# Splitting the mixers' weights ahead of time: hi and lo halves made during the feed-forwards, kept in DRAM and loaded back

## The chip, the cores and the metric

The kernel runs on one NeuronCore of a Trainium2 chip. Its engines work side by side, each through its own queue in order: TensorE (PE in the profile) multiplies matrices into the accumulators in PSUM, VectorE (DVE), ScalarE (ACT) and GpSimd (POOL) work element by element, and SyncE (SP) issues all the DMA transfers of this kernel. The metric is the device time of one execution in microseconds, as the median of several runs.

## What is computed

Two decoder layers on 512 tokens of width 1024. Each layer adds half a SwiGLU feed-forward, a token mixer, and half a second feed-forward to the residual x. Layer 0 mixes with retention and dilated attention side by side ("hybrid"), layer 1 with stick-breaking attention ("stick").

```python
def swiglu_ffn(x, g, w_in, w_out):
    h = rms_norm(x, g)
    gate, up = jnp.split(h @ w_in, 2, axis=-1)
    return (jax.nn.silu(gate) * up) @ w_out          # w_in 1024 x 5632, w_out 2816 x 1024
...
for layer in range(DEPTH):
    x = x + 0.5 * swiglu_ffn(x, ffn1_norm[layer], ffn1_w_in[layer], ffn1_w_out[layer])
    if layer % 2 == 0:
        x = x + retention_dilated_mixer(x, mix_norm[layer], hyb_w_in[e], ret_gn[e], hyb_w_out[e])
    else:
        x = x + stick_breaking_mixer(x, mix_norm[layer], sb_w_in[o], sb_w_out[o])
    x = x + 0.5 * swiglu_ffn(x, ffn2_norm[layer], ffn2_w_in[layer], ffn2_w_out[layer])
return rms_norm(x, final_norm)
```

All is float32. The mixers' inner parts (rotary embedding, decay, softmax, cumulative log-sums) are written out in the kernel; for this change only their projections with `hyb_w_in`, `hyb_w_out`, `sb_w_in` and `sb_w_out` matter.

## The kernel before

**Three products for one.** Each float32 operand of a projection is cut into a high part, rounded to the matmul type fp32r, and a low part, the rest. `mm3` (L139) then issues three matmuls per 128 x 128 block of weights: hi by hi (L141), hi by lo (L142), lo by hi (L143). Activations lie transposed in SBUF, 128 features by 512 tokens a tile, already split (`hh`, the `o` chunks, the feed-forward's `us`).

**A unit of weights** is a tile of 128 partitions by up to 1024 columns. `weight` (L121) makes one: SP loads the raw tile (`wraw`, four buffers), ACT casts it into `hi` (`whi`, two buffers, L128), and an engine subtracts, lo = raw - hi (`wlo`, two buffers, L129). That engine is `lo_eng[0]`: VectorE in the feed-forwards, GpSimd in the two mixers (L688 and L695 switch to it, L690 and L697 back). A full unit of 1024 columns feeds 24 matmuls of 512 columns.

**Order of the stages:** feed-forward 1 of layer 0, `hybrid`, feed-forward 2 of layer 0, feed-forward 1 of layer 1, `stick`, feed-forward 2 of layer 1. A feed-forward is `ffn` (22 steps f, each a gate unit and an up unit with 24 matmuls apiece, silu, product, split of the result into `u`) and `out_ffn` (8 steps d, each with three units of 8, 7 and 7 blocks, the residual add L215 and the next norm L175).

**A mixer** starts with projections (`hybrid`: four gate units `hyb_g`; `stick`: the first q and k) and then runs eight head pairs. `prep(i+1)` projects q, k and, every second pair, v of the next pair; q and k of the hybrid go through `qk_rot` (L437: a shuffle of the PSUM result L441, products L443 and L444, a sum L445) and are packed by `pack_q` (L392, with ACT L399, L400 and DVE L401) and `pack_k` (L376, DVE L381 and L382). Then the core of pair i runs: `retention_core` (scores into PSUM at L409, times decay at L470, split at L146 and L147), `dilated_core` (softmax with L508, L512, transposes L519), or `stick_core` (ACT L593 and L90, DVE L596, split L151 and L152, then matmuls L617). `attend` (L411) multiplies with the values at L420 and adds the halves at L425. `out_mix` (L279) projects the outputs with 8 units of 640 columns and 4 of 768. GpSimd also splits the output chunks' lo (L152 from `split_v`) and scales the rotary tables (L452); these are not touched.

**Order in the queues.** The program is a plain unrolled Python trace. A planner orders each engine's queue from program order, estimated durations and the buffers that are free, and sets every semaphore; no order is written by hand around the change.

Of the kernel before, what the change touches and what calls it, by code (L numbers as in the profile page):

```python
# [20 lines left out]
P = 128  # L21
# [13 lines left out]
def trunk(ctx: ExitStack, tc: tile.TileContext, a: dict, out: bass.AP):  # L35
    nc = tc.nc
    cpool = ctx.enter_context(tc.tile_pool(name="cpool", bufs=1))
    wraw = ctx.enter_context(tc.tile_pool(name="wraw", bufs=4))
    whi = ctx.enter_context(tc.tile_pool(name="whi", bufs=2))
    wlo = ctx.enter_context(tc.tile_pool(name="wlo", bufs=2))  # L40
    hpool = ctx.enter_context(tc.tile_pool(name="hpool", bufs=1))
    big = ctx.enter_context(tc.tile_pool(name="big", bufs=1))
    tmp = ctx.enter_context(tc.tile_pool(name="tmp", bufs=1))
# [77 lines left out]
    def weight(src, cols, pieces=None):  # L121

        raw = wraw.tile([P, 1024], F32, tag="wraw", name=nm("wraw"))
        hi = whi.tile([P, 1024], F32R, tag="whi", name=nm("whi"))
        lo = wlo.tile([P, 1024], F32R, tag="wlo", name=nm("wlo"))
        if pieces is None:
            nc.sync.dma_start(raw[:, :cols], src)
            nc.scalar.copy(out=hi[:, :cols], in_=raw[:, :cols])  # L128
            lo_eng[0].tensor_tensor(out=lo[:, :cols], in0=raw[:, :cols], in1=f32(hi[:, :cols]), op=ALU.subtract)  # L129
        else:  # L130
            for c0, c1, then in pieces:
                nc.sync.dma_start(raw[:, c0:c1], src[:, c0:c1])
                then()
            for c0, c1, _ in pieces:
                nc.scalar.copy(out=hi[:, c0:c1], in_=raw[:, c0:c1])
                nc.vector.tensor_tensor(out=lo[:, c0:c1], in0=raw[:, c0:c1], in1=f32(hi[:, c0:c1]), op=ALU.subtract)
        return hi, lo

    def mm3(ps, whl, col, rhs_hi, rhs_lo, first, last):  # L139
        h, l = whl  # L140
        nc.tensor.matmul(ps, h[:, col:col + P], rhs_hi, start=first, stop=False)  # L141
        nc.tensor.matmul(ps, h[:, col:col + P], rhs_lo, start=False, stop=False)  # L142
        nc.tensor.matmul(ps, l[:, col:col + P], rhs_hi, start=False, stop=last)  # L143
# [51 lines left out]
        return hpool.tile([P, SEQ], F32, tag="ss", name=nm("ss"))  # L195

    def proj_tile(src, ps, w=None):
        w = w or weight(src, D)
        for k in range(KC):
            mm3(ps, w, k * P, hh[k][:, 0, :], hh[k][:, 1, :], k == 0, k == KC - 1)  # L200

# [13 lines left out]
        nc.vector.scalar_tensor_tensor(out=x[d][:, sl], in0=ps[:, sl], scalar=0.5, in1=x[d][:, sl],  # L215
                                       op0=ALU.mult, op1=ALU.add)

    def out_ffn(w_out, us, gcol):

        ss = norm_start()  # L220
        act_set(LNEXP)
        for d in range(KC):
            ps = ACC()
            out_tile(w_out[d], ps, us)
            add_half(d, ps)
            norm_chunk(d, gcol, ss)
# [52 lines left out]
    def out_mix(wa, wb, chunks, gcol):  # L279

        ss = norm_start()
        for d in range(KC):
            ps = ACC()
            w = weight(wa[d], 640)
            for f in range(5):
                mm3(ps, w, f * P, chunks[f][:, 0, :], chunks[f][:, 1, :], f == 0, f == 4)
            nc.vector.tensor_add(out=x[d], in0=ps, in1=x[d])
        for d in range(KC):
            if d % 2 == 0:
                w = weight(wb[d // 2], 768)  # L290
            ps = ATT()
            for f in range(3):
                mm3(ps, w, (d % 2) * 384 + f * P, chunks[5 + f][:, 0, :], chunks[5 + f][:, 1, :], f == 0, f == 2)
            nc.vector.tensor_add(out=x[d], in0=ps, in1=x[d])
            norm_chunk(d, gcol, ss)
        return ss

    def ffn(r, w_in, first=None, pieces=None):

        us = []  # L300
        for f in range(FC):
            pg = ACC()
# [29 lines left out]
    def values(wsrc, rtm):  # L332

        pv = [ACC(), ACC()]
        for u in range(2):
            h, l = weight(wsrc[u], 1024)
            for kk in range(4):
                k = 4 * u + kk
                wh, wl = h[:, kk * 256:kk * 256 + 256], l[:, kk * 256:kk * 256 + 256]
                for t in range(NB):  # L340
                    hi, lo = hh[k][:, 0, t * P:(t + 1) * P], hh[k][:, 1, t * P:(t + 1) * P]
                    o = pv[t // 2][:, (t % 2) * 256:(t % 2) * 256 + 256]
                    nc.tensor.matmul(o, hi, wh, start=k == 0 and t % 2 == 0, stop=False, skip_group_check=True)  # L343
# [186 lines left out]
    def hybrid(ss, gcol_next):  # L530
        gates = []
        for p in range(4):
            ps = ACC()
            proj_tile(a["hyb_g"][p], ps)
            if p == 0:
                r = norm_r(ss)
                rtm = token_r(r)
                act_set(SILU)
            g = T()
            nc.vector.tensor_mul(out=g, in0=ps, in1=r)  # L540
            if p % 2 == 0:
# [10 lines left out]
        def prep(i):  # L552
            p = i % 4
            if i < 4:
                if p % 2 == 0:
                    vs[i // 2] = values(a["hyb_rv"][p // 2], rtm)
                return (qk_rot(a["hyb_rq"][p], rot_r, sw_r, pack_q), qk_rot(a["hyb_rk"][p], rot_r, sw_r, pack_k))
            if p % 2 == 0:
                vs[i // 2] = values(a["hyb_dv"][p // 2], rtm)
            return (qk_rot(a["hyb_dq"][p], rot_d, sw_d, lambda y: pack_q(y, -0.125)),  # L560
                    qk_rot(a["hyb_dk"][p], rot_d, sw_d, pack_k))

        ready = prep(0)
        for i in range(8):
# [7 lines left out]
                retention_core(i, q, k, vs[i // 2], gates[i], outs, bd)  # L572
            else:
                dilated_core(i - 4, q, k, vs[i // 2], dmask, outs)
        return out_mix(a["hyb_oa"], a["hyb_ob"], outs, gcol_next)

    def stick_core(p, q, k, v, cm, outs, idr, tri, nones):
        banks = {}
# [53 lines left out]
        outs.append(oo)  # L632

    def stick(ss, gcol_next):
        first = [project(a["sb_q"][0]), project(a["sb_k"][0])]
        r = norm_r(ss)
        rtm = token_r(r)
        r8 = T(tag="r2")
# [9 lines left out]

        def prep(p, ps=None):
            if p and p % 2 == 0:  # L650
                vs[p // 2] = values(a["sb_v"][p // 2], rtm)
            qp, kp = ps or (project(a["sb_q"][p]), project(a["sb_k"][p]))
            return qk_plain(qp, r8, pack_q), qk_plain(kp, r, pack_k)

        ready = prep(0, first)
        vs[0] = values(a["sb_v"][0], rtm)
        for p in range(8):
            q, k = ready
            if p < 7:
# [23 lines left out]
            norm_sum(c, ss)  # L683
        return norm_r(ss)

    us = ffn(sums, a["f1_in"][0], first, [(c, c + 512, lambda: None) for c in (0, 512)])
    ss = out_ffn(a["f1_out"][0], us, 8)
    lo_eng[0] = nc.gpsimd  # L688
    ss = hybrid(ss, 16)
    lo_eng[0] = nc.vector  # L690
    us = ffn(lambda: norm_r(ss), a["f2_in"][0])
    ss = out_ffn(a["f2_out"][0], us, 24)
    us = ffn(lambda: norm_r(ss), a["f1_in"][1])
    ss = out_ffn(a["f1_out"][1], us, 32)
# [130 lines left out]
```

## Time and profile before

| what | value |
|---|---|
| median of 3 runs | 2083.76 us (2082.23 to 2086.93) |
| the profiled execution's own time | 2081.9 us |
| its span, first to last instruction | 2080.0 us |
| feed-forward 1, layer 0 | to about 373 us |
| hybrid mixer | about 373 to 687 us |
| the two feed-forwards between the mixers | about 687 to 1412 us |
| stick mixer | about 1412 to 1712 us |
| feed-forward 2, layer 1 | from about 1712 us |
| raw loads of 512 KB, issue to landing | 3.4 us |
| HBM read / written | 182.88 MB / 2.10 MB |

A span of the profile counts from the first instruction; the execution's own time has 1.9 us around it. In the rows of a window, "PE busy (x)" is busy time with the number of instructions that start there; two instructions in flight at once count once. Matmuls overlap: one is listed with about 390 ns but a new one of 512 columns starts about every 227 ns, so the pace of TensorE is read from the count in a stretch that it fills.

### The profile page before, as it was taken

To read this page: it belongs to the slowest core of one execution; us is meant where nothing else is said; L and a number is where in the kernel's file an instruction comes from. 1 tells how busy PE (TensorE), PEld (TensorE's weight loads), DVE (VectorE), ACT (ScalarE), POOL (GpSimd) and SP (SyncE) were. 2 spreads that over 40 slices of the span, in tenths; PEclk is the share of its full clock that TensorE was granted. 3 is DMA by queue.
4 is the path that set the end of the run, shared out by engine and by line. 5 is a ranking of instruction groups with operands and counts; after the bars stand their busy time and mean duration, and the time that the engine had idled before them with its cause. 6 is when DMAs were issued, how large, how long until landed. Compare 5 with 4: busy or idle time off the path is not lost.

```text
span 2080.0 us, 23646 instructions
## 1 busy us (share of the span) xinstructions
PE 1999.6 (96%) x9440; PEld 1662.7 (80%) x9440; DVE 1113.3 (54%) x1640; ACT 769.8 (37%) x1124; POOL 196.4 (9%) x104
## 2 busy tenths in 40 slices
PE   8999999987889999999999999999898999999997
PEld 7888888876667788888888888888777778888887
DVE  6444433378987644443344444336777874444334
ACT  5323332334445423233233323225655653232323
POOL 0000000532223000000000000003322220000000
PEclk9999999999999999999999999999999999999999
DMA  5223333312112332333332323332111032223333
GB/s 183 100 93 100 95 94 100 116 62 71 58 35 71 102 101 92 101 88 100 97 101 91 102 96 92 101 97 75 61 42 46 28 100 91 100 93 101 93 92 125
DMA packets 55695, 186.51 MB, mean 90 GB/s; under 512 B 6304, under 2 KB 7072, under 8 KB 55584
## 3 DMA queue, kind: packets, MB, share of 16 engines
q1 hardware_dynamic: 55584, 185.00, 28.0%
q8 instruction: 74, 1.21, 0.2%
q14 instruction: 37, 0.30, 0.0%
HBM read 182.88 MB, written 2.10 MB: 89 GB/s over the span
## 4 chain that ended last, share of the span: by engine, by line
PE 84%; DVE 12%; ACT 3%; issue 1%; DMA 0%; SPq 0%; DVEq 0%; ACTq 0%
PE acc L142 18%; PE acc L143 18%; PE acc L141 18%; PE att L141 8%; PE att L142 8%; PE att L143 8%; PE att L617 2%; PE po L420 2%; DVE qk L381 1%; ACT t L90 1%; DVE tp L444 1%; PE acc L345 1%; PE acc L344 1%; PE acc L343 1%; DVE qk L382 1%
## 5 line engine op out<-in xcount | busy, mean ns | idle before, releaser
L128 ACT CAST whi<-wraw 128x1024 fp32r<-128x1024 f32 (+3 forms) x352 | 356.3, 1012 | 1007.9 <-PE acc L142 550.4
L129 DVE TENSOR_TENSOR wlo<-wraw,whi 128x1024 fp32r<-128x1024 f32 (+1 forms) x276 | 328.5, 1190 | 238.9 <-ACT whi L128 236.9
L141 PE MATMUL acc<-h,whi 128*128 128x512 f32 x992 | 390.6, 394 | 6.0 <-ACT h L174 6.0
L142 PE MATMUL acc<-h,whi 128*128 128x512 f32 x992 | 389.8, 393 | 0.9 <-DVE h L175 0.6
L143 PE MATMUL acc<-h,wlo 128*128 128x512 f32 x992 | 390.0, 393 | 0.0
L129 POOL TENSOR_TENSOR wlo<-wraw,whi 128x1024 fp32r<-128x1024 f32 (+2 forms) x76 | 167.4, 2202 | 1436.6 <-ACT whi L128 1376.8
L141 PE MATMUL att<-h,whi 128*128 128x512 f32 x704 | 275.1, 391 | 0.0
L143 PE MATMUL att<-h,wlo 128*128 128x512 f32 x704 | 274.3, 390 | 0.0
L142 PE MATMUL att<-h,whi 128*128 128x512 f32 x704 | 273.9, 389 | 0.0
L141 PEld LDWEIGHTS acc<-h,whi 128*128 128x128 f32 x992 | 187.8, 189 | 44.9 <-ACT h L174 5.9
L142 PEld LDWEIGHTS acc<-h,whi 128*128 128x128 f32 x992 | 187.7, 189 | 41.1 <-DVE h L175 3.6
L143 PEld LDWEIGHTS acc<-h,wlo 128*128 128x128 f32 x992 | 187.6, 189 | 39.0 <-issue 0.7
L315 DVE TENSOR_TENSOR tp<-att,r 128x512 f32<-128x512 f32 x88 | 60.9, 692 | 281.4 <-PE att L143 281.4
L309 DVE TENSOR_TENSOR tp<-acc,r 128x512 f32<-128x512 f32 x88 | 60.9, 692 | 183.6 <-PE acc L143 183.4
L141 PEld LDWEIGHTS att<-h,whi 128*128 128x128 f32 x704 | 132.3, 188 | 28.0 <-issue 0.7
L142 PEld LDWEIGHTS att<-h,whi 128*128 128x128 f32 x704 | 132.0, 188 | 27.9 <-issue 0.7
L143 PEld LDWEIGHTS att<-h,wlo 128*128 128x128 f32 x704 | 132.1, 188 | 27.8 <-issue 0.2
L141 PE MATMUL acc<-o,whi 128*128 128x512 f32 (+1 forms) x352 | 135.3, 384 | 0.0
L142 PE MATMUL acc<-o,whi 128*128 128x512 f32 (+1 forms) x352 | 134.8, 383 | 0.0
L143 PE MATMUL acc<-o,wlo 128*128 128x512 f32 (+1 forms) x352 | 134.3, 382 | 0.0
L141 PEld LDWEIGHTS acc<-o,whi 128*128 128x128 f32 x352 | 66.5, 189 | 11.7
L142 PEld LDWEIGHTS acc<-o,whi 128*128 128x128 f32 x352 | 66.5, 189 | 11.7
(179 smaller groups left out, 2960.0 us busy)
## 6 DMA issues: line engine op xcount, KB each, us to landing
wraw<-f_in SPq DMA_DIRECT2D x174, 512.0 KB, 3.4
wraw<-f_out SPq DMA_DIRECT2D x68, 448.0 KB, 3.3
wraw<-f_out SPq DMA_DIRECT2D x34, 512.0 KB, 3.5
wraw<-sb_q SPq DMA_DIRECT2D x8, 512.0 KB, 3.4
wraw<-sb_k SPq DMA_DIRECT2D x8, 512.0 KB, 3.4
wraw<-sb_v SPq DMA_DIRECT2D x8, 512.0 KB, 3.4
wraw<-hyb_oa SPq DMA_DIRECT2D x8, 320.0 KB, 2.8
wraw<-sb_oa SPq DMA_DIRECT2D x8, 320.0 KB, 2.8
```

Of the source, the lines that this page charges most:

```text
L90: r = nc.scalar.activation(out=o, in_=i, func=f, **kw)
L128: nc.scalar.copy(out=hi[:, :cols], in_=raw[:, :cols])
L129: lo_eng[0].tensor_tensor(out=lo[:, :cols], in0=raw[:, :cols], in1=f32(hi[:, :cols]), op=ALU.subtract)
L141: nc.tensor.matmul(ps, h[:, col:col + P], rhs_hi, start=first, stop=False)
L142: nc.tensor.matmul(ps, h[:, col:col + P], rhs_lo, start=False, stop=False)
L143: nc.tensor.matmul(ps, l[:, col:col + P], rhs_hi, start=False, stop=last)
L309: nc.vector.tensor_mul(out=t1, in0=pg, in1=rr)
L315: nc.vector.tensor_mul(out=t2, in0=pu, in1=rr)
L343: nc.tensor.matmul(o, hi, wh, start=k == 0 and t % 2 == 0, stop=False, skip_group_check=True)
L344: nc.tensor.matmul(o, hi, wl, start=False, stop=False, skip_group_check=True)
L420: nc.tensor.matmul(po[:, SEQ - n:], st, banks[b][:, c, at:at + n], start=j == 0 and c == 0, stop=j == NB - 1 and c == 1, skip_group_check= ...
L617: nc.tensor.matmul(z[:, at + n - m:at + n], st, sp[:, c, s0:s0 + m], start=False, stop=i == len(adds) - 1 and c == 1, skip_group_check=True)
```

## The change

During the first three feed-forwards each step also makes one unit of the next mixer's weights (`cut_ahead`): the usual load, cast on ACT and subtraction on VectorE, and then two DMA writes, of hi and of lo, into a DRAM tile. In the mixers `unit` finds such a tile and `weight_cut` loads it: in turn into one `whl` buffer with one DMA, or into two `wraw` buffers with two DMAs. The pools `whi` and `wlo` (two buffers each of 4 KB a partition) become one pool `whl` of three buffers that hold hi and lo together (8 KB).

28 hybrid units (all but its output projection) are cut in the first feed-forward, at steps f = 2 to 21 of `ffn` and d = 0 to 7 of `out_ffn`; all 36 stick units in the next two, 18 in each `ffn`. The hybrid's 12 output units still go through `weight`; as `lo_eng` is not switched any more, VectorE subtracts them. GpSimd keeps its other work.

```diff
-    whi = ctx.enter_context(tc.tile_pool(name="whi", bufs=2))
-    wlo = ctx.enter_context(tc.tile_pool(name="wlo", bufs=2))
+    whl = ctx.enter_context(tc.tile_pool(name="whl", bufs=3))
+    dram = ctx.enter_context(tc.tile_pool(name="dram", bufs=1, space=bass.MemoryType.DRAM))
...
-        hi = whi.tile([P, 1024], F32R, tag="whi", name=nm("whi"))
-        lo = wlo.tile([P, 1024], F32R, tag="wlo", name=nm("wlo"))
+        hl = whl.tile([P, 2, 1024], F32R, tag="whl", name=nm("whl"))
+        hi, lo = hl[:, 0, :], hl[:, 1, :]
...
+    def cut_ahead(key, cols):
...
+        hi, lo = weight(src, cols)
+        keep = dram.tile([P, 2, cols], F32, tag="cut_" + "_".join(map(str, key)), name="cut_" + "_".join(map(str, key)))
+        for i, part in enumerate((hi, lo)):
+            nc.sync.dma_start(keep[:, i, :], f32(part[:, :cols]))
+        cut[key] = keep
...
+    def weight_cut(key, cols):
...
+        turns[0] += 1
+        keep = cut[key]
+        if turns[0] % 2:
+            hl = whl.tile([P, 2, 1024], F32R, tag="whl", name=nm("whl"))
+            nc.sync.dma_start(f32(hl[:, :, :cols]), keep)
+            return hl[:, 0, :], hl[:, 1, :]
+        hl = [wraw.tile([P, 1024], F32R, tag="wraw", name=nm("wcut")) for _ in range(2)]
+        for i in range(2):
+            nc.sync.dma_start(f32(hl[i][:, :cols]), keep[:, i, :])
+        return hl
+
+    def unit(key, cols):
+        if key in cut:
+            return weight_cut(key, cols)
...
             norm_chunk(d, gcol, ss)
+            if ahead:
+                cut_ahead(*ahead.pop(0))
...
             us.append(u)
+            if ahead and f > 1:
+                cut_ahead(*ahead.pop(0))
...
-    us = ffn(sums, a["f1_in"][0], first, [(c, c + 512, lambda: None) for c in (0, 512)])
-    ss = out_ffn(a["f1_out"][0], us, 8)
-    lo_eng[0] = nc.gpsimd
+    us = ffn(sums, a["f1_in"][0], first, [(c, c + 512, lambda: None) for c in (0, 512)], hyb)
+    ss = out_ffn(a["f1_out"][0], us, 8, hyb)
     ss = hybrid(ss, 16)
-    lo_eng[0] = nc.vector
-    us = ffn(lambda: norm_r(ss), a["f2_in"][0])
+    half = sb[:18]
+    us = ffn(lambda: norm_r(ss), a["f2_in"][0], ahead=half)
     ss = out_ffn(a["f2_out"][0], us, 24)
-    us = ffn(lambda: norm_r(ss), a["f1_in"][1])
+    half = sb[18:]
+    us = ffn(lambda: norm_r(ss), a["f1_in"][1], ahead=half)
     ss = out_ffn(a["f1_out"][1], us, 32)
-    lo_eng[0] = nc.gpsimd
     ss = stick(ss, 40)
-    lo_eng[0] = nc.vector
```

In the mixers each call `weight(a["sb_q"][p], ...)` and the like becomes `unit(("sb_q", p), ...)`; `hyb` and `sb` list the units in the order of their use.

More of the change, by code (lines that the diff above doesn't have):

```diff
@@ L137, in weight, with mm3 @@
         return hi, lo
-    def mm3(ps, whl, col, rhs_hi, rhs_lo, first, last):
-        h, l = whl
+    cut = {}
+    def cut_ahead(key, cols):
+        src = a[key[0]]
+        for i in key[1:]:
+            src = src[i]
+        hi, lo = weight(src, cols)
[3 more added lines that the diff above has]
+        cut[key] = keep
+    turns = [0]
+    def weight_cut(key, cols):
[12 more added lines that the diff above has]
+            return weight_cut(key, cols)
+        src = a[key[0]]
+        for i in key[1:]:
+            src = src[i]
+        return weight(src, cols)
+    def mm3(ps, w, col, rhs_hi, rhs_lo, first, last):
+        h, l = w
         nc.tensor.matmul(ps, h[:, col:col + P], rhs_hi, start=first, stop=False)
@@ L197, in proj_tile @@
     def proj_tile(src, ps, w=None):
-        w = w or weight(src, D)
+        w = w or (unit(src, D) if isinstance(src, tuple) else weight(src, D))
         for k in range(KC):
@@ L216, in add_half, with out_ffn @@
                                        op0=ALU.mult, op1=ALU.add)
-    def out_ffn(w_out, us, gcol):
+    def out_ffn(w_out, us, gcol, ahead=None):
         ss = norm_start()
@@ L283, in out_mix @@
             ps = ACC()
-            w = weight(wa[d], 640)
+            w = unit((wa, d), 640)
             for f in range(5):
@@ L289, in out_mix @@
             if d % 2 == 0:
-                w = weight(wb[d // 2], 768)
+                w = unit((wb, d // 2), 768)
             ps = ATT()
@@ L296, in out_mix, with ffn @@
         return ss
-    def ffn(r, w_in, first=None, pieces=None):
+    def ffn(r, w_in, first=None, pieces=None, ahead=None):
         us = []
@@ L335, in values @@
         for u in range(2):
-            h, l = weight(wsrc[u], 1024)
+            h, l = unit((*wsrc, u), 1024)
             for kk in range(4):
@@ L533, in hybrid @@
             ps = ACC()
-            proj_tile(a["hyb_g"][p], ps)
+            proj_tile(("hyb_g", p), ps)
             if p == 0:
@@ L555, in prep @@
                 if p % 2 == 0:
-                    vs[i // 2] = values(a["hyb_rv"][p // 2], rtm)
-                return (qk_rot(a["hyb_rq"][p], rot_r, sw_r, pack_q), qk_rot(a["hyb_rk"][p], rot_r, sw_r, pack_k))
+                    vs[i // 2] = values(("hyb_rv", p // 2), rtm)
+                return (qk_rot(("hyb_rq", p), rot_r, sw_r, pack_q), qk_rot(("hyb_rk", p), rot_r, sw_r, pack_k))
             if p % 2 == 0:
-                vs[i // 2] = values(a["hyb_dv"][p // 2], rtm)
-            return (qk_rot(a["hyb_dq"][p], rot_d, sw_d, lambda y: pack_q(y, -0.125)),
-                    qk_rot(a["hyb_dk"][p], rot_d, sw_d, pack_k))
+                vs[i // 2] = values(("hyb_dv", p // 2), rtm)
+            return (qk_rot(("hyb_dq", p), rot_d, sw_d, lambda y: pack_q(y, -0.125)),
+                    qk_rot(("hyb_dk", p), rot_d, sw_d, pack_k))
         ready = prep(0)
@@ L574, in hybrid @@
                 dilated_core(i - 4, q, k, vs[i // 2], dmask, outs)
-        return out_mix(a["hyb_oa"], a["hyb_ob"], outs, gcol_next)
+        return out_mix("hyb_oa", "hyb_ob", outs, gcol_next)
     def stick_core(p, q, k, v, cm, outs, idr, tri, nones):
@@ L634, in stick @@
     def stick(ss, gcol_next):
-        first = [project(a["sb_q"][0]), project(a["sb_k"][0])]
+        first = [project(("sb_q", 0)), project(("sb_k", 0))]
         r = norm_r(ss)
@@ L650, in prep @@
             if p and p % 2 == 0:
-                vs[p // 2] = values(a["sb_v"][p // 2], rtm)
-            qp, kp = ps or (project(a["sb_q"][p]), project(a["sb_k"][p]))
+                vs[p // 2] = values(("sb_v", p // 2), rtm)
+            qp, kp = ps or (project(("sb_q", p)), project(("sb_k", p)))
             return qk_plain(qp, r8, pack_q), qk_plain(kp, r, pack_k)
         ready = prep(0, first)
-        vs[0] = values(a["sb_v"][0], rtm)
+        vs[0] = values(("sb_v", 0), rtm)
         for p in range(8):
@@ L661, in stick @@
             stick_core(p, q, k, vs[p // 2], cm, outs, idr, tri, nones)
-        return out_mix(a["sb_oa"], a["sb_ob"], outs, gcol_next)
+        return out_mix("sb_oa", "sb_ob", outs, gcol_next)
     gains = const("gains", 60)
@@ L684, in sums @@
         return norm_r(ss)
-    us = ffn(sums, a["f1_in"][0], first, [(c, c + 512, lambda: None) for c in (0, 512)])
-    ss = out_ffn(a["f1_out"][0], us, 8)
-    lo_eng[0] = nc.gpsimd
+    hyb = [(("hyb_g", p), D) for p in range(4)]
+    for n in "rd":
+        for p in range(4):
+            if p % 2 == 0:
+                hyb += [((f"hyb_{n}v", p // 2, u), D) for u in range(2)]
+            hyb += [((f"hyb_{n}q", p), D), ((f"hyb_{n}k", p), D)]
+    sb = []
+    for p in range(8):
+        sb += [(("sb_q", p), D), (("sb_k", p), D)]
+        if p % 2 == 0:
+            sb += [(("sb_v", p // 2, u), D) for u in range(2)]
+    sb += [(("sb_oa", d), 640) for d in range(8)] + [(("sb_ob", d), 768) for d in range(4)]
+    us = ffn(sums, a["f1_in"][0], first, [(c, c + 512, lambda: None) for c in (0, 512)], hyb)
+    ss = out_ffn(a["f1_out"][0], us, 8, hyb)
     ss = hybrid(ss, 16)
-    lo_eng[0] = nc.vector
-    us = ffn(lambda: norm_r(ss), a["f2_in"][0])
+    half = sb[:18]
+    us = ffn(lambda: norm_r(ss), a["f2_in"][0], ahead=half)
     ss = out_ffn(a["f2_out"][0], us, 24)
-    us = ffn(lambda: norm_r(ss), a["f1_in"][1])
+    half = sb[18:]
+    us = ffn(lambda: norm_r(ss), a["f1_in"][1], ahead=half)
     ss = out_ffn(a["f1_out"][1], us, 32)
-    lo_eng[0] = nc.gpsimd
     ss = stick(ss, 40)
-    lo_eng[0] = nc.vector
     us = ffn(lambda: norm_r(ss), a["f2_in"][1])
```

## The prediction

> **What bounds the kernel now.** First the page's engine rows and the three rows of line L128 and L129, the making of hi and lo.
>
> ```profile
> PE 1999.6 (96%) x9440; PEld 1662.7 (80%) x9440; DVE 1113.3 (54%) x1640; ACT 769.8 (37%) x1124; POOL 196.4 (9%) x104
> ...
> L128 ACT CAST whi<-wraw 128x1024 fp32r<-128x1024 f32 (+3 forms) x352 | 356.3, 1012 | 1007.9 <-PE acc L142 550.4
> L129 DVE TENSOR_TENSOR wlo<-wraw,whi 128x1024 fp32r<-128x1024 f32 (+1 forms) x276 | 328.5, 1190 | 238.9 <-ACT whi L128 236.9
> ...
> L129 POOL TENSOR_TENSOR wlo<-wraw,whi 128x1024 fp32r<-128x1024 f32 (+2 forms) x76 | 167.4, 2202 | 1436.6 <-ACT whi L128 1376.8
> ```
>
> TensorE is busy for 96%: at most 80 us of 2080 could come back from its idle time. GpSimd is busy for 9% and binds nothing by itself. So I read by stage: one feed-forward, the middle of the hybrid, another feed-forward, the middle of stick.
>
> ```profile
> core 0: us, PE busy (x) PEld busy (x) DVE busy (x) ACT busy (x) POOL busy (x), PEclk, DMA share, GB/s
> ...
> 18.00:373.00 355.00, 355.00 (x1565) 293.34 (x1564) 154.18 (x181) 108.02 (x131) 4.79 (x2) 1.00 0.32 102
> ...
> 428.00:666.00 238.00, 201.15 (x1047) 166.72 (x1047) 196.46 (x385) 107.03 (x207) 68.74 (x35) 0.94 0.18 56
> ...
> 687.00:1047.00 360.00, 360.00 (x1587) 297.75 (x1588) 155.37 (x182) 109.08 (x133) 0.00 (x0) 1.00 0.31 97
> ...
> 1437.00:1690.00 253.00, 227.72 (x1283) 191.83 (x1282) 201.31 (x386) 146.10 (x271) 68.67 (x35) 1.00 0.15 47
> ```
>
> The feed-forwards are bound by TensorE alone: no idle time, 360/1587 = 0.227 us a matmul, VectorE 43% busy. In the mixers TensorE idles 238 - 201.15 = 36.9 us (hybrid) and 253 - 227.72 = 25.3 us (stick), and VectorE is 83% and 80% busy. What TensorE waits for there, from the waits of TensorE in the two mixers:
>
> ```profile
> PE att L409 <- DVE t L470: 17.6, 4, 7.7
> PE att L409 <- DVE t L508: 8.0, 4, 4.0
> ...
> PE att L617 <- DVE sp L151: 19.0, 9, 2.9
> ```
>
> These three groups, 44.6 of the 62.2 us, wait for VectorE, not for a weight and not for GpSimd. But GpSimd is behind it. First a place in the hybrid's timeline; then VectorE's instructions grouped by shape, three groups of the hybrid and the last of stick:
>
> ```profile
> 471.02 0.69 DVE L443 TENSOR_TENSOR tp<-acc,o 128x512 f32<-128x512 f32 x1
> ...
> 471.30 2.34 POOL L129 TENSOR_TENSOR wlo<-wraw,whi 128x1024 fp32r<-128x1024 f32 x1 [4.31 <-ACT whi L128]
> ...
> 471.63 2.56 DVE L444 TENSOR_TENSOR tp<-tp,o 128x512 f32<-128x512 f32 x1
> ```
>
> ```profile
> L444 DVE TENSOR_TENSOR tp<-tp,o 128x512 f32<-128x512 f32 x8 | 14.7, 1839 | 0.0
> ...
> L381 DVE CAST qk<-tp 64x512 fp32r<-64x512 f32 x16 | 9.3, 580 | 0.3
> L443 DVE TENSOR_TENSOR tp<-acc,o 128x512 f32<-128x512 f32 x8 | 5.5, 684 | 0.1
> ...
> L381 DVE CAST qk<-tp 64x512 fp32r<-64x512 f32 x16 | 20.2, 1265 | 0.5
> ```
>
> L443 and L444 have the same size. L443 reads one operand from PSUM and takes 0.69 us even while GpSimd subtracts; L444 reads both from SBUF, starts inside a GpSimd subtraction and ends with it, 2.56 us. Over its eight instructions that costs 8 x (1.839 - 0.684) = 9.2 us. The cast L381 suffers in the same way.
>
> **The change, part by part.**
>
> *GpSimd's subtractions go* (all 76, 167.4 us). What that gives TensorE I read from its largest gap: VectorE's rows before it, then the gap.
>
> ```profile
> 418.77 2.61 DVE L444 TENSOR_TENSOR tp<-tp,o 128x512 f32<-128x512 f32 x1
> ...
> 422.14 2.95 DVE L381 CAST qk<-tp 64x512 fp32r<-64x512 f32 x2
> ...
> 427.84 0.68 DVE L444 TENSOR_TENSOR tp<-tp,o 128x512 f32<-128x512 f32 x1
> ...
> 433.33 2.55 DVE L444 TENSOR_TENSOR tp<-tp,o 128x512 f32<-128x512 f32 x1
> ...
> 437.08 0.86 DVE L381 CAST qk<-tp 64x512 fp32r<-64x512 f32 x2
> ...
> 437.21 0.58 PE L409 MATMUL att<-qk,qk 128*128 128x256 f32 x1 [7.74 <-DVE t L470]
> ```
>
> Undisturbed, L444 takes 0.68 and the pair of casts 0.86. The three stretched rows hold 1.9 + 2.1 + 1.9 = 5.9 us too much, and VectorE has no slack between them: the gap of 7.74 would be 1.8, 76% less. Not every gap is so pure (some end after short waits for ACT, and part of the stretching comes from GpSimd's L152 and L452, which stay), so I take 70% of the hybrid's 36.9: **26 us**. The ends are 0 and 36.9. In stick:
>
> ```profile
> 1437.44 2.97 DVE L381 CAST qk<-tp 64x512 fp32r<-64x512 f32 x2
> ...
> 1439.07 1.12 ACT L90 ACTIVATE t<-t,one 128x512 f32<-128x512 f32 x2
> ...
> 1443.29 0.44 PE L617 MATMUL att<-sp,tri 128*128 128x384 f32 x1 [2.56 <-DVE sp L151]
> ```
>
> The casts lose 2.97 - 0.86 = 2.1 us. ACT's logarithms, needed next, end at 1440.2, while VectorE takes them up at 1441.9 (behind L382), so 1.7 of the gap's 2.56 can go, two thirds. The smaller gaps hang more on ACT; I take 55% of 25.3: **14 us**, between 0 and 25.3.
>
> *The clock.* The hybrid stage has a granted clock of 0.94: 0.06 x 238 = 14 us of clock lost, partly in idle time. Two stretches of ten microseconds after gaps, and a smaller gap:
>
> ```profile
> 433.00:443.00 10.00, 5.79 (x28) 5.70 (x29) 9.87 (x18) 1.98 (x4) 2.34 (x1) 0.54 0.15 52
> ...
> 493.00:503.00 10.00, 7.91 (x45) 6.95 (x44) 9.71 (x16) 2.97 (x5) 2.38 (x1) 0.86 0.15 52
> ```
>
> ```profile
> 500.34 0.69 PE L409 MATMUL att<-qk,qk 128*128 128x384 f32 x1 [2.09 <-DVE t L165]
> ```
>
> In the first, TensorE worked 58% of the time. Of the 14 us some 58%, 8 us, was thus lost to work, and it goes with the gaps: 70% is **6 us**, between 0 and 14.
>
> [...]
>
> *Twelve subtractions move to VectorE* in the hybrid's output projection: at most 12 x 1.19 = 14 us, nearer 10, as they are 640 and 768 columns wide. VectorE has 42 us free in that stage and gains more there, so most lies in its idle time; I charge **2 us**, between 0 and 14.
>
> *64 casts, 64 subtractions and 128 writes join the feed-forwards.* The first gets 28: VectorE 154 + 28 x 1.19 = 187 of 355 us, ACT 108 + 28 = 136. TensorE's work there hides both. What would be late without that cover is the next unit's lo. How much room it has:
>
> ```profile
> 769.47 1.05 ACT L128 CAST whi<-wraw 128x1024 fp32r<-128x1024 f32 x1 [3.85 <-issue]
> ...
> 771.06 1.22 DVE L129 TENSOR_TENSOR wlo<-wraw,whi 128x1024 fp32r<-128x1024 f32 x1
> ```
>
> A buffer comes free, and 772.28 - 769.47 = 2.8 us later the next unit is ready. A unit lasts TensorE 24 x 0.227 = 5.4 us, so 2.6 us are free. A cut unit's cast and subtraction, 1.05 + 1.22 = 2.3 us, fit even when they come right in front.
>
> The queues: SP's write of lo waits for the subtraction, and the next raw loads stand behind it. A step f takes 48 x 0.227 = 10.9 us and uses three of four raw buffers, so loads run ahead by more than such a wait. Bytes per step: three loads and two writes of 0.524 MB, 2.62 MB in 10.9 us, 240 GB/s instead of 97. Does the queue carry that, and are writes slower? The output's writes, and the window in which four follow each other:
>
> ```profile
> wraw<-f_in SPq DMA_DIRECT2D x174, 512.0 KB, 3.4
> ...
> outT<-tp SPq DMA_DIRECT2D x4, 256.0 KB, 2.0
> ```
>
> ```profile
> 2058.00:2062.50 4.50, 2.63 (x23) 2.42 (x22) 4.50 (x11) 2.00 (x4) 0.00 (x0) 1.00 0.60 233
> ```
>
> They land in 2.0 us, and 233 GB/s took a DMA share of 0.60. So 240 GB/s is 0.62 by this row, 0.75 by the feed-forward's 0.31 at 97: loads arrive later but in time. Charge: **1 us** in all, from 0 to the 64 x 2.3 = 147 us that all of them in TensorE's way would cost.
>
> In the mixers 64 casts (about 65 us of ACT) vanish and loads double to 1.05 MB a unit; three `whl` buffers and two `wraw` pairs hold up to five units, 27 us of work. I add nothing for ACT.
>
> Sum: 26 + 14 + 6 - 2 - 1 = **43 us**. The profiled execution's 2081.9 becomes 2038.9; the median shown is 1.9 above it, so I forecast 2041.
>
> **The rivals.**
>
> *More comes back.* ACT's 65 us free the chains that my 55% and 70% leave, and every gap and the clock return: 36.9 + 25.3 + 8 = 70 us, 2014 us. For it: casts of weights stand in ACT's queue ahead of work for the mixer. Against: pairs remain chained through ACT, VectorE and TensorE.
>
> *Little comes back.* VectorE's backlog hides waits for ACT and for scores that surface when it is gone; a third of the 43 remains, 15 us, 2069. For it: not a single mixer stage is bound by one engine throughout.
>
> *The loads come late.* A mixer's loads stand in SP's queue behind transfers that wait for other buffers; two thirds of a microsecond at each of the 64 units take the 43 us back: 2084, no change. Against it: five units of lead. This is also how the change could fail to do what it says.
>
> *Slower: the cut units wait for buffers.* A cut's cast on ACT needs one of three `whl` buffers, and a buffer that was cut is free only when its write has landed. Queued behind the cast stand silu, the cast of u and the next unit's cast, for which TensorE waits. A wait of w costs TensorE w - 2.6 us; the gain is gone at 43/64 = 0.7 us a cut, so it decides from w = 3.3 us. At 4.5 us it costs 64 x 1.9 = 122 us: 2163. Against it: cast, subtraction, two issues and a landing of 2.0 to 3.4 us hold a buffer some 6 of the 10.9 us, and two buffers remain for the stream, as before.
>
> **How the numbers follow.** Forecast 0.62 (its own range 2024 to 2058), more 0.10, little 0.13, late loads 0.06, slower 0.09. The range 2012 to 2073 leaves out the slower case, most of the late loads and an edge of the others, about 0.2. Faster by over 0.2% (what a measurement of this kernel can tell from no change): 0.62 + 0.10 + 0.13 = 0.85; same 0.06; slower 0.09.
>
> **What would show it.** In the new profile L444 and L381 should have means near 0.7 and 0.43 us; the GpSimd rows of L129 should be gone and POOL be busy for some 29 us; TensorE's idle time in the mixers should be 20 to 25 us in place of 62, the hybrid's clock above 0.97; the feed-forwards should keep 0.227 us a matmul with a DMA share near 0.7. Wrong would be: idle time of TensorE in the feed-forwards behind ACT's cast or a lo, a wait for a DMA of the cut weights, or gaps of the old size behind VectorE although its instructions are short.

## The result, and the profile after

The changed kernel takes 2022.24 us (median of 4 runs, 2021.98 to 2023.37) against 2082.99 of the kernel before beside it: a ratio of 0.9706, 95% interval 0.9689 to 0.9723, some 61 us less. The profiled execution took 2022.33 us, its span is 2020.3. Its page begins:

```profile
span 2020.3 us, 23997 instructions
...
PE 1988.6 (98%) x9440; PEld 1657.1 (82%) x9440; DVE 1120.3 (55%) x1716; ACT 766.7 (38%) x1124; POOL 28.6 (1%) x28
...
L129 DVE TENSOR_TENSOR whl<-wraw,whl 128x1024 fp32r<-128x1024 f32 (+3 forms) x352 | 411.9, 1173 | 269.4 <-ACT whl L128 268.6
```

VectorE makes all 352 subtractions, 76 more than before. They take 411.9 us in place of 328.5, 83 us of added work, and yet its busy time grew by only 7 us: some 76 us of stretched instructions went. GpSimd is left with 28.6 us.

The stages of the changed kernel, in the columns used before (a feed-forward, the middle of the hybrid, the middle of stick):

```profile
420.00:630.00 210.00, 202.57 (x1093) 168.77 (x1092) 178.69 (x404) 91.27 (x191) 10.97 (x8) 0.99 0.33 112
...
651.00:1010.00 359.00, 359.00 (x1583) 296.96 (x1582) 177.37 (x200) 125.10 (x150) 0.00 (x0) 1.00 0.53 177
...
1401.00:1633.00 232.00, 224.91 (x1273) 190.87 (x1272) 172.85 (x383) 123.87 (x244) 10.31 (x8) 1.00 0.29 98
```

TensorE's idle time is 210 - 202.57 = 7.4 us in the hybrid (36.9 before) and 232 - 224.91 = 7.1 in stick (25.3 before); the hybrid's clock went from 0.94 to 0.99. The feed-forward keeps its pace, 359/1583 = 0.227 us a matmul, with VectorE and ACT busier and nearly twice the bytes (177 GB/s in place of 97). VectorE's rows that were stretched, grouped by shape (two of the hybrid, the last of stick):

```profile
L423 DVE CAST qk<-tp 64x512 fp32r<-64x512 f32 x16 | 7.2, 451 | 0.4
...
L486 DVE TENSOR_TENSOR tp<-tp,o 128x512 f32<-128x512 f32 x8 | 5.5, 693 | 0.0
...
L423 DVE CAST qk<-tp 64x512 fp32r<-64x512 f32 x16 | 6.7, 421 | 0.5
```

L486 is the product that was L444: 693 ns in place of 1839; L423 is the cast that was L381: 451 in place of 580, 421 in place of 1265. What TensorE still waits for in the whole program, its five longest sums (the first is one wait of 6.0 us before the change as well):

```profile
PE acc L178 <- ACT h L211: 6.2, 1, 6.2
PE att L659 <- DVE sp L188: 6.1, 7, 1.2
PE att L451 <- DVE t L550: 3.0, 4, 1.9
PE att L451 <- DVE t L512: 2.5, 7, 0.5
PE acc L178 <- DMA whl<-cut_hyb_g: 1.8, 1, 1.8
```

The last row is new: the hybrid's first weights come 1.8 us late. Their 1 MB load is issued at 365.1 us, after a wait for a buffer, and from 360 to 378 us the DMA engines are busy for 0.80 of the time.

To say where the 60 us of span came from, each norm's sum (the matmul with `ones_ms`) serves as a milestone. Before, then after, from the timeline of TensorE:

```profile
374.76 1.02 PE L191 MATMUL po<-ss,ones_ms 128*128 128x512 f32 x2
...
686.90 1.10 PE L191 MATMUL po<-ss,ones_ms 128*128 128x512 f32 x2
...
1412.30 1.02 PE L191 MATMUL po<-ss,ones_ms 128*128 128x512 f32 x2
...
1710.31 1.10 PE L191 MATMUL po<-ss,ones_ms 128*128 128x512 f32 x2
```

```profile
377.21 1.02 PE L228 MATMUL po<-ss,ones_ms 128*128 128x512 f32 x2
...
651.22 1.02 PE L228 MATMUL po<-ss,ones_ms 128*128 128x512 f32 x2
...
1375.63 1.02 PE L228 MATMUL po<-ss,ones_ms 128*128 128x512 f32 x2
...
1652.65 1.10 PE L228 MATMUL po<-ss,ones_ms 128*128 128x512 f32 x2
```

| stretch | before, us | after, us | difference |
|---|---|---|---|
| start to the hybrid's norm | 374.8 | 377.2 | +2.4 |
| hybrid | 312.1 | 274.0 | -38.1 |
| two feed-forwards | 725.4 | 724.4 | -1.0 |
| stick | 298.0 | 277.0 | -21.0 |
| last feed-forward | 369.7 | 367.7 | -2.0 |

The mixers gave it all. The question for the experiments is which part of the change did it: GpSimd's silence, ACT's casts that are gone, VectorE's subtractions that are elsewhere, the third buffer, or the copies in DRAM.

### The profile page after: what moved, and what is told of

Same layout as the page of the kernel before. It is cut to its first block, busy times and chain, and to the rows that moved or that the text cites. A ratio compares the mean times of both kernels' runs of the same rounds, so it can differ in the third digit from the quotient of the medians.

```text
span 2020.3 us, 23997 instructions
## 1 busy us (share of the span) xinstructions
PE 1988.6 (98%) x9440; PEld 1657.1 (82%) x9440; DVE 1120.3 (55%) x1716; ACT 766.7 (38%) x1124; POOL 28.6 (1%) x28
## 4 chain that ended last, share of the span: by engine, by line
PE 89%; DVE 7%; ACT 2%; issue 1%; DMA 1%; SPq 0%; DVEq 0%; ACTq 0%
PE acc L179 18%; PE acc L180 18%; PE acc L178 18%; PE att L180 8%; PE att L179 8%; PE att L178 8%; PE att L659 2%; PE po L462 1%; ACT t L90 1%; PE acc L387 1%; PE acc L386 1%; PE acc L385 1%; DVE qk L424 1%; PE att L451 0%; DVE qlo L443 0%
## 5 line engine op out<-in xcount | busy, mean ns | idle before, releaser
L128 ACT CAST whl<-wraw 128x1024 fp32r<-128x1024 f32 (+3 forms) x352 | 355.2, 1010 | 865.4 <-PE acc L180 491.4
L129 DVE TENSOR_TENSOR whl<-wraw,whl 128x1024 fp32r<-128x1024 f32 (+3 forms) x352 | 411.9, 1173 | 269.4 <-ACT whl L128 268.6
L178 PE MATMUL acc<-h,whl 128*128 128x512 f32 x848 | 332.4, 392 | 8.0 <-ACT h L211 6.2
L179 PE MATMUL acc<-h,whl 128*128 128x512 f32 x848 | 332.2, 392 | 0.0
L180 PE MATMUL acc<-h,whl 128*128 128x512 f32 x848 | 331.2, 391 | 0.0
L178 PE MATMUL att<-h,whl 128*128 128x512 f32 x704 | 274.7, 390 | 0.0
L180 PE MATMUL att<-h,whl 128*128 128x512 f32 x704 | 274.3, 390 | 0.0
L179 PE MATMUL att<-h,whl 128*128 128x512 f32 x704 | 274.3, 390 | 0.0
L178 PEld LDWEIGHTS acc<-h,whl 128*128 128x128 f32 x848 | 160.0, 189 | 41.4 <-ACT h L211 6.2
L179 PEld LDWEIGHTS acc<-h,whl 128*128 128x128 f32 x848 | 159.8, 188 | 33.8 <-DVE h L212 1.4
L180 PEld LDWEIGHTS acc<-h,whl 128*128 128x128 f32 x848 | 159.6, 188 | 32.7 <-issue 0.2
L179 PEld LDWEIGHTS att<-h,whl 128*128 128x128 f32 x704 | 132.1, 188 | 28.3 <-issue 0.7
L180 PEld LDWEIGHTS att<-h,whl 128*128 128x128 f32 x704 | 132.3, 188 | 27.8 <-issue 0.5
L178 PEld LDWEIGHTS att<-h,whl 128*128 128x128 f32 x704 | 132.0, 188 | 27.7 <-issue 0.5
L178 PE MATMUL acc<-o,whl 128*128 128x512 f32 (+1 forms) x332 | 127.6, 384 | 0.0
L180 PE MATMUL acc<-o,whl 128*128 128x512 f32 (+1 forms) x332 | 127.0, 383 | 0.0
L179 PE MATMUL acc<-o,whl 128*128 128x512 f32 (+1 forms) x332 | 126.8, 382 | 0.0
L178 PEld LDWEIGHTS acc<-o,whl 128*128 128x128 f32 x332 | 62.9, 189 | 11.3
L179 PEld LDWEIGHTS acc<-o,whl 128*128 128x128 f32 x332 | 62.8, 189 | 11.3
L180 PEld LDWEIGHTS acc<-o,whl 128*128 128x128 f32 x332 | 62.8, 189 | 11.2
```

## The experiments

The theory from the prediction: GpSimd's subtraction stretches VectorE's instructions, and that was the mixers' idle time. The rivals: ACT's relief, or weights that are ready sooner. Ratios are to the kernel before in the same series.

**GpSimd's work put back**, with nobody waiting for it (`hl` is a unit that was loaded ready):

```diff
+        idle = cpool.tile([P, 960], mybir.dt.bfloat16, tag="idle", name=nm("idle"))
+        n = min(cols, 960)
+        nc.gpsimd.tensor_tensor(out=idle[:, :n], in0=f32(hl[0][:, :n]), in1=f32(hl[1][:, :n]), op=ALU.subtract)
```

> The changed kernel, and for each of the 64 units loaded ready GpSimd subtracts hi minus lo into a scratch tile that nobody reads (960 of the 1024 columns, result in bf16); the output is unchanged. Theory (GpSimd's subtractions stretch VectorE's instructions that read two SBUF operands or cast, and that stretching was the mixers' idle time): 64 x about 2.3 us of GpSimd return, L486 and L423 go back towards 1.5 us and 1 us, TensorE's idle time in the mixers from 15 back to 40 us or more, time 2050 to 2075 us. Rival (the gain comes from ACT's 64 casts that are gone, or from weights that are ready sooner): nobody waits for the scratch tile, time stays within 8 us of the changed kernel, 2022 to 2030.

Measured: 2100.3 us, ratio 1.0075 (1.0052 to 1.0098). The theory's side, but outside its 2050 to 2075: the whole gain is lost and 0.75% besides. Its hybrid and stick stages, one group of GpSimd, and VectorE's rows of the hybrid (L427 the cast, L490 the product):

```profile
418.00:668.00 250.00, 216.40 (x1118) 181.82 (x1117) 214.93 (x411) 93.54 (x195) 54.04 (x26) 0.92 0.28 98
1439.00:1713.00 274.00, 243.71 (x1272) 206.08 (x1271) 206.79 (x383) 123.60 (x243) 65.78 (x34) 0.92 0.24 83
```

```profile
L169 POOL TENSOR_TENSOR idle<-whl 128x960 bf16<-128x960 f32 x26 | 63.4, 2438 | 1100.9 <-DMA whl<-cut_sb_q 731.2 <-DMA whl<-cut_hyb_g 367.8
```

```profile
L427 DVE CAST qk<-tp 64x512 fp32r<-64x512 f32 x16 | 17.0, 1062 | 0.4
...
L490 DVE TENSOR_TENSOR tp<-tp,o 128x512 f32<-128x512 f32 x8 | 9.9, 1241 | 0.0
```

TensorE idles 33.6 and 30.3 us, the clock falls to 0.92 in both mixers, and the stretched rows are back. The two waits that decide between theory and rival:

```profile
PE att L455 <- DVE t L516: 25.1, 4, 8.8
...
PE acc L182 <- DMA whl<-cut_hyb_g: 1.7, 1, 1.7
```

TensorE waits for VectorE again, and for a weight only once, 1.7 us, as in the changed kernel; so GpSimd's extra reading of the buffers made no weight late. The weights are ready here and ACT is relieved; neither keeps the gain. Why stick is even longer than before (319.6 us against 298.0), while the hybrid is back at its old length (312.6), was not followed up.

**ACT's work put back**, and separately **VectorE's**, and **both chained**, each into the same scratch tile:

```diff
+        nc.scalar.copy(out=idle[:, :n], in_=f32(hl[0][:, :n]))
```

> The changed kernel, and for each of the 64 units loaded ready ACT copies hi into a scratch tile that nobody reads (960 of the 1024 columns, result in bf16); the output is unchanged. So ACT has its 65 us back in the mixers and GpSimd has nothing. Theory (GpSimd against VectorE): VectorE's durations stay short, 2022 to 2032 us. Rival (ACT's casts stood in the mixers' chains): 2040 to 2060 us, with TensorE's gaps behind VectorE rows that wait for ACT.

Measured: 2026.4 us, 0.9721 (0.9696 to 0.9746), some 4 us over the changed kernel, with intervals that overlap. So ACT's casts are worth little as long as they wait for nothing but a landed load.

```diff
+        nc.vector.tensor_tensor(out=idle[:, :n], in0=f32(hl[0][:, :n]), in1=f32(hl[1][:, :n]), op=ALU.subtract)
```

> The changed kernel, and for each of the 64 units loaded ready VectorE subtracts hi minus lo into a scratch tile that nobody reads (960 of the 1024 columns, result in bf16), some 64 x 1.1 = 70 us of VectorE in the mixers; the output is unchanged. It prices the place of the subtraction. Theory (in the mixers VectorE's time is TensorE's time, whether it is work or stretching): the kernel before with VectorE subtracting took 2057, of which ACT's casts are 4; so 2045 to 2055 us. Rival (VectorE has room once GpSimd is quiet): 2022 to 2032, and then it is the late weights of that kernel that cost.

Measured: 2026.6 us, 0.9717 (0.9700 to 0.9735). The theory of this run fell: once GpSimd's subtractions are gone, VectorE has room for 64 in the mixers, if they too wait only for a landed load.

```diff
+        nc.scalar.copy(out=idle[:, :n], in_=f32(hl[0][:, :n]))
+        nc.vector.tensor_tensor(out=idle[:, :n], in0=f32(hl[0][:, :n]), in1=idle[:, :n], op=ALU.subtract)
```

> The changed kernel, and for each of the 64 units loaded ready ACT copies hi into a scratch tile and VectorE subtracts that tile from hi (960 columns, bf16); nobody reads the result and the output is unchanged. So both engines do a cast and a subtraction per unit, chained, as soon as a load has landed, but no buffer of TensorE holds them up. Theory C (waiting for buffers costs, not the work): 2024 to 2036 us. Theory D (cast and subtraction together fill the engines): 2045 to 2058.

Measured: 2025.5 us, 0.9703 (0.9687 to 0.9719), not to be told from the changed kernel. In its hybrid stage VectorE is busy for a larger share than in the kernel before (196.46 of 238 there), and yet TensorE idles only 9.2 us:

```profile
420.00:630.00 210.00, 200.81 (x1088) 166.49 (x1087) 195.80 (x424) 107.19 (x208) 11.10 (x7) 0.99 0.33 111
```

So the busy share of VectorE was no sign of a bound by itself; it depends on what hangs on the instructions.

**Only the engine changed:** the kernel before without the two switches to GpSimd.

```diff
-    lo_eng[0] = nc.gpsimd
     ss = hybrid(ss, 16)
-    lo_eng[0] = nc.vector
...
-    lo_eng[0] = nc.gpsimd
     ss = stick(ss, 40)
-    lo_eng[0] = nc.vector
```

> The kernel before, with VectorE subtracting the mixers' weights as in the feed-forwards; no DRAM copies. GpSimd's 76 subtractions are gone as in the change, but VectorE takes 76 more in the mixers, 64 x 1.19 + 12 x 0.85 = 86 us. Theory: VectorE loses about as much stretching (some 70 us) as it gains in work, so that a part of the gain remains: 2055 to 2080 us. Rival (VectorE's total in the mixers is the bound): no change or slower, 2083 to 2110. If nearly all the gain is there (under 2035), neither the moving of work nor ACT's relief was needed.

Measured: 2057.3 us, 0.9869 (0.9847 to 0.9890), as expected: some 25 of the 60 us. But not for the reason given there, as the two runs on VectorE's work show. The product takes 685 ns again. What is left was looked for in ACT's queue, where the cast of the next weights waits for a buffer. First the hybrid stage of this kernel and that wait of ACT, then a place in its timeline:

```profile
428.00:656.00 228.00, 205.77 (x1044) 167.21 (x1043) 191.15 (x408) 104.47 (x205) 13.01 (x8) 0.93 0.18 59
```

```profile
ACT whi L128 <- PE acc L142: 29.5, 14, 4.4
```

```profile
467.69 2.27 DVE L470 TENSOR_TENSOR t<-att,o 128x512 f32<-128x512 f32 x5
...
467.98 1.05 ACT L128 CAST whi<-wraw 128x1024 fp32r<-128x1024 f32 x1 [3.64 <-PE acc L142]
468.93 1.14 ACT L146 CAST ah<-t 128x512 fp32r<-128x512 f32 x2
```

The cast of the next weights stands 3.64 us at the head of ACT's queue until TensorE has finished with a buffer, and the splits of the attention scores (L146), for which TensorE waits in turn, stand behind it. At this place that costs them little: the products that they split (L470) begin only at 467.69, so they lose at most 1.2 us. The two longest gaps of TensorE in this stretch, 2.10 and 2.12 us, have another row in front, a cast of VectorE beside one of the subtractions that GpSimd keeps. Before the first of them:

```profile
490.75 1.79 POOL L152 TENSOR_TENSOR o<-t,o 128x512 fp32r<-128x512 f32 x1 [33.02 <-DVE o L151]
...
491.40 1.42 DVE L381 CAST qk<-tp 64x512 fp32r<-64x512 f32 x1
```

If waiting for a buffer is the rest all the same, a third buffer must bring it back.

```diff
-    whi = ctx.enter_context(tc.tile_pool(name="whi", bufs=2))
-    wlo = ctx.enter_context(tc.tile_pool(name="wlo", bufs=2))
+    whi = ctx.enter_context(tc.tile_pool(name="whi", bufs=3))
+    wlo = ctx.enter_context(tc.tile_pool(name="wlo", bufs=3))
```

> The kernel before with VectorE subtracting the mixers' weights (2057 us) and three buffers in each of the pools for hi and lo. The added work alone cost 4 us each on ACT and on VectorE when it hung on nothing but a landed load, while making the weights in the mixers costs 35 us over the changed kernel. Theory C (what costs is that a cast must wait at the head of ACT's queue, and the subtraction behind it on VectorE, for TensorE to free a buffer): a third buffer loosens it, 2035 to 2050 us. Theory D (the work costs when cast and subtraction come together, wherever they wait): 2053 to 2060.

Measured: 2028.4 us, 0.9718 (0.9702 to 0.9734), a larger gain than either theory allowed. Its hybrid stage and the same wait of ACT:

```profile
428.00:640.00 212.00, 201.21 (x1091) 167.12 (x1090) 198.74 (x421) 110.15 (x215) 11.44 (x8) 1.00 0.21 68
```

```profile
ACT whi L128 <- PE acc L142: 20.3, 12, 3.9
```

TensorE idles 10.8 us in place of 22.2, the clock is full, and this wait of ACT is down by a third. The whole hybrid, from norm to norm, with two buffers and then with three:

```profile
374.80:676.70 301.90, 279.67 (x1418) 229.95 (x1417) 240.39 (x479) 139.31 (x253) 19.04 (x12) 0.95 0.20 68
```

```profile
374.70:650.30 275.60, 264.81 (x1420) 221.33 (x1419) 239.35 (x479) 138.46 (x253) 17.47 (x12) 1.00 0.23 75
```

It is 26.3 us shorter: 11.4 us of idle time, and 14.9 us by which the same matmuls run faster at the fuller clock. In stick the third buffer brings nothing clear (285.4 and 284.2 us). Of the idle time in the hybrid, TensorE's waits behind L425 (5.3 us in all) and for weights that came late (2.8 us) are gone. That waiting for buffers costs here, and not the work, is shown by this run together with the one in which both engines had the work back (2025.5 us); which queue carries the wait to TensorE is not shown.

With no copy in DRAM this kernel has all of the gain but some 5 us of span (2025.6 against 2020.3), and the intervals of the two ratios overlap. So 64 units cut ahead, through copies in DRAM, buy no more than that. What they buy lies in stick, 277.0 us against 284.2; but that stage varies from 277 to 283 us over the other runs with units loaded ready and without GpSimd's subtractions, so this is not clear of scatter.

**The third buffer alone:** the kernel before, GpSimd subtracting, with the same edit of the pools.

> The kernel before with three buffers in each of the two pools for hi and lo in place of two, as many as the changed kernel has; nothing else. The cuts alone took 2095, 12 us over the kernel before, with the feed-forwards unchanged and stick 12 us longer. Theory A (the third buffer shifts the order of GpSimd's subtractions against VectorE's work in stick): 2088 to 2098. Theory B (something of the cuts reaches into stick): 2078 to 2085.

Measured: 2084.0 us, 0.9993 (0.9975 to 1.0011): nothing. While GpSimd's subtractions stretch VectorE's instructions (the product L444 takes 1838 ns here, 1839 in the kernel before), a third buffer is of no use here.

**The cuts alone:** the changed kernel, whose mixers do as before.

```diff
-        if key in cut:
-            return weight_cut(key, cols)
...
+    lo_eng[0] = nc.gpsimd
     ss = hybrid(ss, 16)
+    lo_eng[0] = nc.vector
```

(the same around `stick`).

> The changed kernel with all cuts and writes in the feed-forwards, but the mixers make their weights as in the kernel before (load, cast on ACT, subtraction on GpSimd) and read none of the DRAM copies; the output is unchanged. It prices the cuts alone, with the three-buffer pool. Theory (TensorE hides the cuts): 2078 to 2088 us. Rival (the cuts cost and a larger gain covered it): 2095 us or more, with TensorE's idle time in the first three feed-forwards.

Measured: 2094.8 us, 1.0049 (1.0029 to 1.0068), outside what the theory allowed. But the feed-forwards did not pay it; the second one before, then here with 18 units cut in it:

```profile
689.00:1046.00 357.00, 357.00 (x1577) 295.61 (x1576) 154.23 (x182) 107.23 (x130) 0.00 (x0) 1.00 0.31 97
```

```profile
691.00:1048.00 357.00, 357.00 (x1577) 295.61 (x1576) 177.06 (x200) 123.81 (x149) 0.00 (x0) 1.00 0.51 177
```

The same 1577 matmuls in the same 357 us, with 18 more subtractions and 18 more casts. By the milestones the loss lies in stick (310.4 us against 298.0), where nothing is cut. The third buffer alone had cost nothing, so the joint pool of hi and lo was left as a cause:

```diff
-    whi = ctx.enter_context(tc.tile_pool(name="whi", bufs=2))
-    wlo = ctx.enter_context(tc.tile_pool(name="wlo", bufs=2))
+    whl = ctx.enter_context(tc.tile_pool(name="whl", bufs=3))
...
+        hl = whl.tile([P, 2, 1024], F32R, tag="whl", name=nm("whl"))
+        hi, lo = hl[:, 0, :], hl[:, 1, :]
```

> The kernel before with one pool of three buffers that hold hi and lo together, as in the changed kernel; no cuts. The cuts alone took 2095 with this pool; two pools of three took the time of the kernel before. Theory A (the joint pool reorders GpSimd's subtractions in stick): 2088 to 2098. Theory B (the cuts reach into stick): 2078 to 2087.

Measured: 2091.5 us, 1.0025 (1.0013 to 1.0038), with 309.9 us in stick. The ratio speaks of some 5 us, not of 12, and in the profile of the third buffer alone stick took 303.3 us at an unchanged time, so part of the 12 us is scatter between executions. What is left of stick's loss comes with the joint pool where GpSimd subtracts, and the cuts cost the feed-forwards nothing. Why the joint pool orders GpSimd's subtractions worse there was not followed up; nor were the 2 us by which the hybrid of the cuts alone is longer (314.7 us, against 312.4 here).

**GpSimd busy, but reading nothing:**

```diff
+        for _ in range(2):
+            nc.gpsimd.memset(idle[:, :n], 0.0)
```

> The changed kernel, and for each of the 64 units loaded ready GpSimd sets a scratch tile to zero twice (960 columns of bf16) as soon as that tile is free; the output is unchanged. GpSimd is busy but reads nothing. Theory 1 (VectorE is held only while GpSimd reads SBUF operands): 2020 to 2028 us, VectorE's two-operand rows stay at 0.69 us. Theory 2 (any GpSimd instruction that touches SBUF holds VectorE): some 1 to 2 us per unit, 2035 us or more.

Measured: 2022.0 us, 0.9695 (0.9675 to 0.9715). The time decides nothing on the mixers: as the memsets wait for no load, the planner put them in the first 120 us. They answer in part all the same. From 20 to 100 us GpSimd is busy for 75 us, and VectorE's subtractions, which read two SBUF operands, take what they take beside a quiet GpSimd; the stretch, then the subtractions in it:

```profile
20.00:100.00 80.00, 80.00 (x353) 65.90 (x352) 48.12 (x56) 32.11 (x39) 75.15 (x85) 1.00 0.67 229
```

```profile
L129 DVE TENSOR_TENSOR whl<-wraw,whl 128x1024 fp32r<-128x1024 f32 x22 | 26.9, 1222 | 6.9 <-ACT whl L128 6.9
```

1222 ns each; in the changed kernel the same 22 took 1223. These GpSimd instructions, which only write, did not hold them. No cast of VectorE ran in that stretch, so for casts this is open.

**The rest of GpSimd's subtractions to VectorE** (the output chunks' lo, L189):

```diff
-        split_v(oo[:, 0, :], oo[:, 1, :], o, nc.gpsimd)
+        split_v(oo[:, 0, :], oo[:, 1, :], o)
```

> The changed kernel with the last 16 GpSimd subtractions (the output chunks' lo, L189, 1.33 us each) on VectorE (0.69 us each); GpSimd keeps only the rotary tables. Theory: VectorE gains 16 x 0.69 = 11 us of work and loses what is left of the stretching, some 5 to 10 us: 2016 to 2026 us, within 0.2% either way. A clear gain would say that the remaining gaps still come from GpSimd.

Measured: 2018.95 us, 0.9683 (0.9666 to 0.9700), the lowest time of all these kernels; but its interval overlaps that of the changed kernel, so a gain is not shown.

```diff
+            if more:
+                cut_ahead(*more.pop(0))
...
-    ss = out_ffn(a["f1_out"][0], us, 8, hyb)
+    ss = out_ffn(a["f1_out"][0], us, 8, hyb, [(("hyb_oa", d), 640) for d in range(8)])
```

> The changed kernel with the output chunks' lo on VectorE (2019 us), and 8 of the hybrid's 12 output units cut ahead too, a second one in each step of the first out_ffn. Theory: VectorE has room now, so 8 subtractions of 0.81 us fewer in the hybrid give at most 3 us: 2014 to 2021 us. Rival (more writes in out_ffn delay its loads or the first load of the mixer): 2022 or more.

Measured: 2023.7 us, 0.9693 (0.9675 to 0.9711): above the theory's range and in the rival's, but the interval overlaps that of the kernel without the eight. No gain from cutting more.

## Why the prediction was right, and where it was too small

The direction, the range and the main mechanism held: 2041 was forecast within 2012 to 2073, and 2022 was measured. A gain of 43 us was forecast, one of some 60 came. That is 2 us below the forecast's own range (2024 to 2058) and nearer to the rival "More comes back" (2014 us, chance 0.10) than to the forecast: the stated range held because it reached out for that rival. The rival's reason, ACT's 65 us, is not what the runs show, since ACT's casts put back cost some 4 us. By norm-to-norm stages, of the 17 us that were missing about 9 are idle time of TensorE in the mixers (49 us went, 40 were forecast), 4 its faster matmuls (10 against 6), and 4 the charges (3 were set, none came). By the prediction's own steps:

- **GpSimd's subtractions stretch VectorE.** Shown twice: with them gone the product takes 693 ns and the casts 451 and 421, as forecast (0.7 and 0.43 us); with them put back and nothing else, the whole gain is lost. Two readings of rows were off, without harm to the sum: L444 at 471.63 does not end with GpSimd's subtraction (473.64) but 0.55 us behind it, and all eight products of the hybrid that take 2.16 to 2.65 us end 0.54 or 0.55 us behind the L129 of GpSimd beside them, so with 0.68 us undisturbed they look held until then rather than slowed; and between the stretched rows before the gap of 7.74 us VectorE did have slack, two waits for ACT of 0.69 and 0.61 us.
- **The share of the idle time that would go** was set at 70% in the hybrid and 55% in stick, from one dissected gap each. Measured: 36.9 to 7.4 (80%) and 25.3 to 7.1 (72%), 29.4 and 18.2 us in place of 26 and 14. The shares were set lower than the gaps shown for the sake of waits behind ACT; most of those went too.
- **The clock** was set at 6 us. Over the whole hybrid TensorE's busy time, with the same matmuls, fell from 274.7 us at a clock of 0.96 to 266.6 at 0.99: the 8 us that the prediction saw in the clock came back in full, not 70% of them. That the 8 is so close is in part luck, since its 58% was read from one stretch, and the other stretch shown has 79%. Stick gave 2.1 us of this kind, which the prediction did not price.
- **The charges.** The twelve subtractions (2 us) and the feed-forwards (1 us) cost nothing visible: the two feed-forwards between the mixers and the last one gave 1.0 and 2.0 us back. The 2.4 us lost ahead of the hybrid's norm are mostly a wait for the first load, 1.8 us, which the rival of late loads had named and which happened once instead of 64 times.
- **What the sum left out:** how the making of the weights waits for buffers. "I add nothing for ACT" holds for ACT's time (some 4 us), and the prediction put the whole return of idle time down to GpSimd. But with GpSimd's subtractions merely given to VectorE, 25 of the 60 us come; another 29 come with the third buffer, which is worth nothing with GpSimd at work. The prediction named casts that stand in ACT's queue only in a rival and priced no wait for a buffer in the mixers. In the changed kernel only the hybrid's twelve output units are still made there. How much of the missing 17 us this explains was not measured.
- **The slower rival** needed a cut to wait 3.3 us for a buffer. It did not come: with the cuts alone, the same matmuls ran in the same 357 us.

The profile after matches the marks set: GpSimd busy 28.6 us (29 forecast), DMA share 0.66 in the first feed-forward (0.7), the hybrid's clock 0.99 (above 0.97). In the stretch of the second feed-forward shown, with 18 units where the first has 28, the share is 0.53. (The prediction's 0.31 at 97 GB/s scales to 0.77 at 240, not 0.75.) The idle time in the mixers fell further, to 14.5 us in place of 20 to 25.

## What to carry to other kernels

An engine that is busy for 9% can be the cause of another's waits: compare the mean duration of a group with that of the same shape elsewhere in the program, and look at what runs beside the long ones. Then try the smallest remedy first: giving the subtraction to VectorE and a third buffer to the weights reached, but for some 5 us of span, what 64 units copied through DRAM reached. And when a wait at the head of a queue looks guilty, check whether what stands behind it was ready: the cast that waited 3.64 us on ACT held up splits whose inputs were not there yet for most of that time.

## What the runs showed of the hardware

A GpSimd subtraction of two SBUF operands stretched VectorE's products of two SBUF operands from 0.69 to about 2.5 us, and a pair of its casts from 0.86 to 2.95, while a product with one operand in PSUM beside it took 0.69. Beside GpSimd's memsets, which only write, VectorE's subtractions of two SBUF operands kept their 1222 ns. What it is that holds VectorE beside a subtraction is not shown.

The clock fell behind gaps of about 2 us. In the run with only the engine changed, no gap of TensorE in the hybrid's middle exceeds 2.12 us, and its clock there is 0.93. One stretch of it, and the two gaps around its start:

```profile
494.48 0.39 PE L409 MATMUL att<-qk,qk 128*128 128x256 f32 x1 [2.10 <-DVE t L470]
...
500.67 1.86 PE L420 MATMUL po<-ah,v 128*128 128x512 f32 x4 [2.01 <-DVE t L425]
```

```profile
498.00:508.00 10.00, 7.99 (x36) 6.91 (x35) 6.10 (x9) 2.29 (x5) 0.00 (x0) 0.66 0.47 157
```

In this stretch matmuls of 256 columns start every 0.21 us from 503.4 to 505.7; from 507.4 on, as at 490, they start every 0.12 us. So the gaps around 500 us were paid twice, in idle time and in slow matmuls behind them; between two and three buffers, over the whole hybrid, the second part came to 14.9 us and the first to 11.4.

In the changed kernel, with two gaps above 0.7 us in that stage (0.73 and 1.92), the stage keeps 0.99; the ten microseconds from 590 us on, with the second, have 0.83. The length of one gap does not decide by itself: in the kernel before, a gap of 3.34 us up to 536.15 left 1.00 from 533 to 543, while the stretch from 493 to 503, with a gap of 2.09 us up to 500.34, has 0.86. What decides is not shown.
